# Mamba decay differences: the 0/1 triangle as the stationary tile, four heads side by side

## The chip, the cores and the metric

The kernel is one program for one core of a Trainium2 chip. The metric is the device time of one execution in microseconds (us); the runs before give 2568.35, 2570.22 and 2571.57 us, median 2570.22 us.

## The reference, cut to what matters

A network of four layers with three sublayers each (FFN, mixer, FFN) on 256 tokens of width 1024, followed by a second block of three sublayers. The mixer of the third layer is Mamba-2. Its scan works on two chunks of 128 tokens, with 32 heads in 4 groups of 8. The part that the change touches is the decay matrix of each head within a chunk:

```python
acum = jnp.cumsum(dtc * a_g, axis=1)
seg = acum[:, :, None] - acum[:, None, :]
decay = jnp.exp(jnp.where(causal, seg, -jnp.inf))
cb = jnp.einsum('blgn,bsgn->blsg', cc, bc)
y = jnp.einsum('blsg,blsgh,bsghp->blghp', cb, decay, xc * dtc[..., None])
```

For token l and source s the difference seg is the sum of dt*a over the tokens after s up to l. Written with two 0/1 triangles it is a matrix product: sum over k of [k > s] * dta[k] * [k <= l].

## The kernel before

All work runs on one core: weights come in float32 by DMA (`raw`), ScalarE rounds them to the short format float32r (`whi`, line 219), VectorE makes the remainder (`wlo`, line 222), and TensorE multiplies three times (hi*hi, hi*lo, lo*hi; lines 252 to 254 and 640 to 642). The work of each sublayer is written as steps, and a string of step names gives the order in which they are issued to a scheduler that may interleave them; buffers come from pools. For the Mamba sublayer the string is `ORDER_MAMBA` (line 114).

The Mamba steps are, for group g, chunk t and half q: `Z` (gate projection, its result `sz` stays until `Y`), `B` and `X` (projection by `feat`, lines 1012 to 1014, then the convolution `conv`: one ScalarE instruction and three on VectorE, lines 1002 and 1005), `tB` and `tX` (transposes; `tX` ends in four VectorE multiplications, line 1065), `S` (state, lines 1073 to 1077), `C` (the 128x128 matrix `cbm`, line 1085), `G` (decay, four heads at a time, lines 1087 to 1096), `Y` (output of the scan, from line 1098), `W` and `O` (output projection). `D` (line 964) computes dt and `dta` once for each chunk.

There are 16 `G` steps. Each has four VectorE instructions that scale the triangle `slow` by one head's column of `dta` into a quarter of the tile `dm`, and four float32 matmuls with that quarter as the stationary tile and the triangle `tri` as the moving one, into a quarter of the PSUM tile `pg`. The trace shows each float32 matmul as two records, each with its own weight load. ScalarE then takes the exponential of the whole `pg` back into `dm` (line 1095), and VectorE multiplies by `cbm` (line 1096). `dm` is one of the 10 buffers of the pool `half` (`NH = 10`), which `sz`, `bct`, `state`, `cacc`, `sx`, `xw`, `yi` and others share; it is held until `Y` has read it (line 1103). `pg` is one of four PSUM buffers with the tag `y`.

Of the kernel before, what the change touches and what calls it, by code (L numbers as in the profile page):

```python
# [10 lines left out]
F32 = mybir.dt.float32  # L11
F32R = mybir.dt.float32r
BF16 = mybir.dt.bfloat16
I32 = mybir.dt.int32
AF = mybir.ActivationFunctionType
OP = mybir.AluOpType
AX = mybir.AxisListType

P = 128
# [144 lines left out]
class Net:  # L164
# [783 lines left out]
    def mamba(self, x, done):  # L948
        nc, A = self.nc, self.A
# [9 lines left out]
        nc.sync.dma_start(cbb, A["ssm_conv_b"])  # L959
        ng = self.cst.tile([P, 16], F32, name="ng")  # L960
        nc.sync.dma_start(ng, A["ssm_norm_g"])
        dt, dta, ea, w, z, ys = {}, {}, {}, {}, {}, []

        def fD(t):
            if "dt" not in w:
                w["dt"] = self.wblock("ssm_w_dt", 0, 0, 1024, 32)
            ps = self.bank("mm", "pdt")
            self.lin(ps[:, :32], x, t, w["dt"], 32)
            u = self.small(32, "u")
            nc.vector.tensor_tensor(u, ps[:, :32], dtb, OP.add)  # L970
            m = self.small(32, "m")
            nc.vector.tensor_scalar(m, u, -1.0, None, op0=OP.mult)
            nc.vector.tensor_tensor(m, m, u, OP.min)
            e = self.small(32, "e")
            nc.scalar.activation(e, m, AF.Exp)
            s = self.small(32, "sden")
            nc.vector.tensor_scalar(s, e, 2.0, None, op0=OP.add)
            nc.vector.reciprocal(s, s)
            nc.vector.tensor_tensor(s, s, e, OP.mult)
            s2 = self.small(32, "s2")  # L980
            nc.vector.tensor_tensor(s2, s, s, OP.mult)
            pl = self.small(32, "pl")
            nc.vector.tensor_scalar(pl, s2, 1.0 / 19, None, op0=OP.mult)
            for k in range(17, 1, -2):
                nc.vector.scalar_tensor_tensor(pl, pl, 1.0 / k, s2, OP.add, OP.mult)
            nc.vector.scalar_tensor_tensor(pl, pl, 1.0, s, OP.add, OP.mult)
            nc.vector.tensor_scalar(u, u, 0.0, None, op0=OP.max)
            d = self.cst.tile([P, 32], F32, name=f"dt{t}")
            nc.vector.scalar_tensor_tensor(d, pl, 2.0, u, OP.mult, OP.add)
            da = self.cst.tile([P, 32], F32, name=f"dta{t}")  # L990
            nc.vector.scalar_tensor_tensor(da, d, -1.0, alog, OP.mult, OP.mult)
            dt[t], dta[t] = d, da

        def tD(t):
            pe = self.bank("tr", "pea")
# [90 lines left out]

        def fG(g, t, q):
            pg = self.bank("y", "pg").rearrange("p (a b) -> p a b", a=4)
            dm = self.half([P, 4, P], name="dm")
            for j in range(4):  # L1090
                h = 8 * g + 4 * q + j
                nc.vector.tensor_scalar(dm[:, j, :], self.slow, dta[t][:, h:h + 1], None, op0=OP.mult)
                nc.tensor.matmul(pg[:, j, :], dm[:, j, :], self.tri, start=True, stop=True)
            ee = z["e", g, t, q] = dm
            nc.scalar.activation(ee, pg, AF.Exp)
            nc.vector.tensor_tensor(ee, ee, self.bc(z["cb", g, t], 4, P), OP.mult)

# [34 lines left out]
        close = self.closers(yy, done)  # L1132
        close["E"] = close.pop("D")
        steps = dict(D=fD, tD=tD, Z=fZ, B=fB, tB=tB, X=fX, tX=tX, S=fS, C=fC, G=fG, Y=fY, W=W, O=O, **close)
        self.go(steps, ORDER_MAMBA)

# [457 lines left out]
```

## Time and profile before

| what | value |
|---|---|
| median of three runs | 2570.22 us (2568.35 to 2571.57) |
| profiled execution, span from first to last instruction | 2567.9 us, 34087 instructions |
| TensorE busy (matmul records) | 2497.5 us, 97% |
| VectorE busy | 2129.1 us, 83% |
| ScalarE busy | 1286.9 us, 50% |
| granted TensorE clock, mean | 0.992 |
| Mamba sublayer in the trace | about 1289 to 1480 us of the span |

For the profiled execution the span is all that is recorded of its time; it is 0.45 us under the lowest of the timed runs and 2.3 us under their median. A busy time counts each instruction from its start to its end, and where two overlap, once. PE is TensorE's matmuls, PEld its weight loads, DVE VectorE, ACT ScalarE.

### The profile page before, as it was taken

The page shows a single profiled execution, that of the slowest core. Times are in us where ns is not written, and L with a number is a line of the kernel's source. Part 1 is how long each engine was busy: PE and PEld are TensorE (multiplying, and loading weights), DVE is VectorE, ACT ScalarE, POOL GpSimd, SP SyncE. Part 2 cuts the span into 40 slices and gives each one's busy share as a digit, 9 for nine tenths or more (in the row PEclk, how much of TensorE's full clock was granted, in tenths as well). Part 3 has the DMA queues.
Part 4 walks back from the last instruction along what each step waited for, and adds up shares of the span by engine and source line. Part 5 has one row for each costly group of instructions (what it writes and reads, how often), then busy time and mean ns, then how long its engine had stood idle before and what let it go on. Part 6 is the DMA issues. An engine that isn't in the chain of part 4 may idle for free.

```text
span 2567.9 us, 34087 instructions
## 1 busy us (share of the span) xinstructions
PE 2497.5 (97%) x12252; PEld 2065.0 (80%) x12252; DVE 2129.1 (83%) x4847; ACT 1286.9 (50%) x2005; POOL 0.2 (0%) x4
## 2 busy tenths in 40 slices
PE   7999899999999999999999999999989999999998
PEld 6788688888887788888889778887878888788887
DVE  7888988879898988898989987698898856896754
ACT  3544474444446544544566554454446544555542
POOL 0000000000000000000000000000000000000000
PEclk9999999999999999999999999999999999999999
DMA  8888457848876388688742457658845754444552
GB/s 309 308 340 306 159 194 276 309 169 300 321 267 256 123 299 320 221 299 316 270 158 99 164 202 292 252 211 324 310 166 211 275 179 175 164 157 172 200 180 80
DMA packets 92297, 599.15 MB, mean 233 GB/s; under 512 B 12768, under 2 KB 14432, under 8 KB 24672
## 3 DMA queue, kind: packets, MB, share of 16 engines
q1 hardware_dynamic: 92128, 596.98, 63.5%
q8 instruction: 96, 1.57, 0.2%
q14 instruction: 73, 0.60, 0.1%
HBM read 593.79 MB, written 3.15 MB: 232 GB/s over the span
## 4 chain that ended last, share of the span: by engine, by line
PE 86%; DVE 7%; DMA 3%; ACT 2%; issue 1%; SPq 0%; DVEq 0%; ACTq 0%
PE tr L263 4%; PE y0q L640 3%; PE y0q L642 3%; PE y0q L641 3%; PE y1q L640 3%; PE y1q L642 3%; PE y1q L641 3%; DVE wlo L222 2%; PE hid0t L254 1%; PE hid6t L253 1%; PE hid9t L252 1%; PE hid6t L254 1%; PE hid9t L254 1%; PE hid6t L252 1%; PE hid5t L254 1%; PE hid9t L253 1%
## 5 line engine op out<-in xcount | busy, mean ns | idle before, releaser
L222 DVE TENSOR_TENSOR wlo<-raw,whi 128x384 fp32r<-128x384 f32 (+1 forms) x2385 | 1081.7, 505 | 145.8 <-ACT whi L219 76.0
L219 ACT ACTIVATE whi<-raw 128x1024 fp32r<-128x1024 f32 (+1 forms) x801 | 820.2, 1051 | 377.3 <-DMA raw<-in_ffn_w_in_dram 133.5
L371 DVE SCALAR_TENSOR_TENSOR acc<-rawm,cond,acc 128x1024 f32<-128x1024 f32 x252 | 322.9, 1281 | 13.2 <-DMA rawm<-in_w_mod_dram 8.0
L640 PE MATMUL y1q<-whi,ah 128*128 128x512 f32 x396 | 161.7, 408 | 1.7 <-ACT ah L625 1.7
L640 PE MATMUL y0q<-whi,ah 128*128 128x512 f32 x396 | 156.2, 394 | 0.7 <-ACT ah L625 0.2
L642 PE MATMUL y1q<-whi,al 128*128 128x512 f32 x396 | 156.4, 395 | 0.0
L641 PE MATMUL y0q<-wlo,ah 128*128 128x512 f32 x396 | 155.2, 392 | 0.0
L642 PE MATMUL y0q<-whi,al 128*128 128x512 f32 x396 | 155.2, 393 | 0.0
L641 PE MATMUL y1q<-wlo,ah 128*128 128x512 f32 x396 | 155.0, 391 | 0.0
L625 ACT ACTIVATE ah<-tr 128x256 fp32r<-128x256 f32 x198 | 74.7, 382 | 139.6 <-PE tr L263 136.7
L626 DVE TENSOR_TENSOR al<-tr,ah 128x256 fp32r<-128x256 f32 x198 | 82.0, 418 | 34.5 <-ACT ah L625 33.9
L640 PEld LDWEIGHTS y0q<-whi,ah 128*128 128x128 f32 x396 | 74.4, 188 | 17.1 <-ACT ah L625 2.6
L642 PEld LDWEIGHTS y1q<-whi,al 128*128 128x128 f32 x396 | 74.4, 188 | 15.7
L640 PEld LDWEIGHTS y1q<-whi,ah 128*128 128x128 f32 x396 | 74.5, 188 | 14.8 <-ACT ah L625 2.4
L642 PEld LDWEIGHTS y0q<-whi,al 128*128 128x128 f32 x396 | 74.3, 188 | 14.9 <-DVE al L626 0.2
L641 PEld LDWEIGHTS y0q<-wlo,ah 128*128 128x128 f32 x396 | 74.4, 188 | 14.5
L641 PEld LDWEIGHTS y1q<-wlo,ah 128*128 128x128 f32 x396 | 74.7, 189 | 13.2
L285 ACT ACTIVATE ev<-tr,B,G 128x128 f32<-128x128 f32 x192 | 72.9, 466 | 20.4 <-PE tr L263 20.3
L263 PEld LDWEIGHTS tr<-k_ident,ac 128*128 128x128 f32 x396 | 54.0, 140 | 29.6 <-DVE ac L616 3.0
L263 PE MATMUL tr<-k_ident,ac 128*128 128x128 f32 x396 | 74.5, 273 | 2.5 <-DVE ac L616 2.0
L295 DVE TENSOR_TENSOR tmp<-ev,tmp 128x512 fp32r<-128x512 f32 (+1 forms) x76 | 50.5, 664 | 12.7 <-ACT tmp L287 11.8
L252 PE MATMUL hid0t<-whi,tmp 128*128 128x512 f32 x144 | 56.4, 392 | 1.9 <-ACT tmp L287 1.9
(510 smaller groups left out, 6006.0 us busy)
## 6 DMA issues: line engine op xcount, KB each, us to landing
raw<-in_ffn_w_in_dram SPq DMA_DIRECT2D x176, 1024.0 KB, 4.9
rawm<-in_w_mod_dram SPq DMA_DIRECT2D x144, 1024.0 KB, 4.8
raw<-in_ffn_w_out_dram SPq DMA_DIRECT2D x88, 1024.0 KB, 5.0
raw<-in_w_gate_up_dram SPq DMA_DIRECT2D x22, 1024.0 KB, 4.7
raw<-in_w_in_dram SPq DMA_DIRECT2D x14, 1024.0 KB, 4.7
raw<-in_diff_w_in_dram SPq DMA_DIRECT2D x12, 1024.0 KB, 4.7
raw<-in_w_down_dram SPq DMA_DIRECT2D x11, 1024.0 KB, 4.7
raw<-in_w_kv_mem_dram SPq DMA_DIRECT2D x8, 1024.0 KB, 6.4
```

The costliest lines, as they stand in the source:

```text
L219: nc.scalar.activation(hi[:, q:e], s[:, q:e], AF.Copy)
L222: nc.vector.tensor_tensor(lo[:, q:e], s[:, q:e], hi[:, q:e].bitcast(F32), OP.subtract)
L252: nc.tensor.matmul(ps, xh, hi[:, off:off + n], start=first, stop=False)
L254: nc.tensor.matmul(ps, xl, hi[:, off:off + n], start=False, stop=last)
L263: self.nc.tensor.transpose(ps[:, j, :], src[:, j * P:(j + 1) * P], self.ident)
L285: nc.scalar.activation(src[:, j, :], ps[:, j, :], AF.Identity, scale=sc, bias=bcols[:, c + j:c + j + 1])
L371: nc.vector.scalar_tensor_tensor(o, src, sc, o, OP.mult, OP.add)
L625: nc.scalar.activation(ah, tr, AF.Copy)
L626: nc.vector.tensor_tensor(al, tr, ah.bitcast(F32), OP.subtract)
L640: nc.tensor.matmul(y[t][q], ah[:, k, :], hi[:, sl], start=f, stop=False)
L641: nc.tensor.matmul(y[t][q], ah[:, k, :], lo[:, sl], start=False, stop=False)
L642: nc.tensor.matmul(y[t][q], al[:, k, :], hi[:, sl], start=False, stop=l)
```

## The change

In step `G` the two operands change places and the scaling is done for four heads in one instruction. A copy of the triangle `slow` in float32r (`slowr`) is now the stationary tile. VectorE multiplies the triangle `tri`, repeated four times, by four columns of `dta`, repeated along the row, into one 128x512 float32r tile, and one 512-column matmul takes it as the moving tile. To keep precision `dta` is split into a short-format part (`dah`) and a remainder (`dal`), so there are two such multiplications and two matmuls that accumulate in `pg`, in place of four scalings and four float32 matmuls. Each of the two moving tiles is a buffer of the pool `half`, and the exponential goes to a third one. The split costs one ScalarE and one VectorE instruction on 128x32 for each chunk, the copy of the triangle one ScalarE instruction on 128x128. `slowr` and the split parts lie in a buffer that the attention of layers one and four uses for `krT`.

```diff
-        dt, dta, ea, w, z, ys = {}, {}, {}, {}, {}, []
+        both = self.fp.tile([P, 256], F32R, tag="krT", name=self.nm("both"), bufs=1)
+        slowr = both[:, :P]
+        nc.scalar.activation(slowr, self.slow, AF.Copy)
+        dt, dta, dhl, ea, w, z = {}, {}, {}, {}, {}, {}
...
-            dt[t], dta[t] = d, da
+            dah, dal = (both[:, P + 64 * t + 32 * c:P + 64 * t + 32 * c + 32] for c in range(2))
+            nc.scalar.activation(dah, da, AF.Copy)
+            nc.vector.tensor_tensor(dal, da, dah.bitcast(F32), OP.subtract)
+            dt[t], dta[t], dhl[t] = d, da, (dah.bitcast(F32), dal.bitcast(F32))
...
         def fG(g, t, q):
             pg = self.bank("y", "pg").rearrange("p (a b) -> p a b", a=4)
-            dm = self.half([P, 4, P], name="dm")
-            for j in range(4):
-                h = 8 * g + 4 * q + j
-                nc.vector.tensor_scalar(dm[:, j, :], self.slow, dta[t][:, h:h + 1], None, op0=OP.mult)
-                nc.tensor.matmul(pg[:, j, :], dm[:, j, :], self.tri, start=True, stop=True)
-            ee = z["e", g, t, q] = dm
+            hs = slice(8 * g + 4 * q, 8 * g + 4 * q + 4)
+            for i in range(2):
+                dm = self.half([P, 4, P], F32R, "dm")
+                nc.vector.tensor_tensor(dm, self.bc(self.tri, 4, P), self.hb(dhl[t][i][:, hs], 4, P), OP.mult)
+                nc.tensor.matmul(pg, slowr, dm, start=i == 0, stop=i == 1)
+            ee = z["e", g, t, q] = self.half([P, 4, P], name="ee")
             nc.scalar.activation(ee, pg, AF.Exp)
             nc.vector.tensor_tensor(ee, ee, self.bc(z["cb", g, t], 4, P), OP.mult)
```

## Rows read from the trace of the kernel before

**Rows 1.** Page, part 1: engine, busy us (share of the span), instructions.
```profile
PE 2497.5 (97%) x12252; PEld 2065.0 (80%) x12252; DVE 2129.1 (83%) x4847; ACT 1286.9 (50%) x2005; POOL 0.2 (0%) x4
```

**Rows 2.** Windows: stretch, length, busy us (count) by engine, clock, DMA share, GB/s.
```profile
1289.40:1336.30 46.90, 46.60 (x330) 43.39 (x328) 39.06 (x115) 31.97 (x41) 0.00 (x0) 0.96 0.51 180
...
1336.30:1471.40 135.10, 130.43 (x870) 115.81 (x870) 126.05 (x362) 81.42 (x120) 0.00 (x0) 1.00 0.36 126
...
1471.40:1480.00 8.60, 8.60 (x38) 7.13 (x39) 4.97 (x15) 2.06 (x4) 0.00 (x0) 1.00 0.29 118
...
1580.00:1600.00 20.00, 20.00 (x92) 16.49 (x91) 13.52 (x30) 10.68 (x14) 0.00 (x0) 1.00 0.86 322
```

**Rows 3.** Groups by shape, 1330 to 1470 us: busy, mean ns, idle before.
```profile
L1093 PE MATMUL pg<-k_tri,dm 128*128 128x128 f32 x128 | 16.1, 279 | 1.6 <-DVE dm L1092 1.6
...
L1092 DVE TENSOR_SCALAR dm<-k_slow,dta 128x128 f32<-128x128 f32 x64 | 13.2, 279 | 0.0
...
L1096 DVE TENSOR_TENSOR dm<-dm,cbm 128x512 f32<-128x512 f32 x16 | 10.5, 684 | 0.5 <-ACT dm L1095 0.4
```

**Rows 4.** Timeline of VectorE, two stretches: start, us, instruction.
```profile
1336.29 3.22 DVE L1092 TENSOR_SCALAR dm<-k_slow,dta 128x128 f32<-128x128 f32 x16
1339.42 2.49 DVE L1096 TENSOR_TENSOR dm<-dm,cbm 128x512 f32<-128x512 f32 x4
1341.94 0.48 DVE L1005 SCALAR_TENSOR_TENSOR cacc<-pbc,cw,cacc 128x253 f32<-128x253 f32 x1
...
1467.30 0.68 DVE L1104 TENSOR_TENSOR xs<-py,xs 128x512 f32<-128x512 f32 x1
...
1469.10 0.68 DVE L1110 TENSOR_TENSOR xs<-xs,yi 128x512 f32<-128x512 f32 x1
1469.70 0.42 DVE L222 TENSOR_TENSOR wlo<-raw,whi 128x256 fp32r<-128x256 f32 x1
```

**Rows 5.** Chain that ended last, first and third burst: start, us, what.
```profile
1336.62 3.84 PE pg L1093 x32
1340.46 2.63 PE py L1103 x24
...
1400.72 1.79 PE pg L1093 x16
```

**Rows 6.** Windows, a stretch of 48 short-format 512-column matmuls; columns as in Rows 2.
```profile
1455.44:1466.31 10.87, 10.87 (x49) 9.01 (x48) 9.35 (x21) 6.61 (x7) 0.00 (x0) 1.00 0.84 295
```

**Rows 7.** Chain that ended last, 1362 to 1374 us.
```profile
1365.13 1.09 PE pg L1093 x8
...
1366.24 0.61 ACT dm L1095
...
1367.76 1.56 DVE dm L1092 x8
...
1370.13 0.61 DVE dm L1096
```

**Rows 8.** Waits, 1336 to 1471 us: who waited for whom, us, times, longest.
```profile
DVE xd L1065 <- PE trx L1060: 4.2, 4, 1.9
...
DVE xs L1104 <- PE py L1103: 1.8, 4, 0.6
...
PE pg L1093 <- DVE dm L1092: 1.6, 3, 0.7
...
PE py L1103 <- DVE dm L1096: 1.4, 2, 0.7
```

**Rows 9.** Small instructions on 128x32: one line's view, and the timeline of ScalarE.
```profile
L991 DVE SCALAR_TENSOR_TENSOR dta<-dt,alog x2: 185/188/192, 1293.7 to 1307.6; 128x32 f32<-128x32 f32 x2
...
1300.77 0.22 ACT L975 ACTIVATE e<-m 128x32 f32<-128x32 f32 x1
1300.89 1.05 ACT L219 ACTIVATE whi<-raw 128x1024 fp32r<-128x1024 f32 x1
```

**Rows 10.** Timeline of ScalarE in the first burst of G steps.
```profile
1341.34 0.56 ACT L1002 ACTIVATE cacc<-pbc,cbb,cw 128x256 f32<-128x256 f32 x1 [0.24 <-DVE dm L1096]
```

## The prediction

> **What bounds the kernel now.** I read the page's engine line first. TensorE is busy 97% of the span and VectorE 83% [rows 1], so over the whole kernel a microsecond taken from TensorE could come off the time. But the change lies in one sublayer, and what it is worth is read there. So next I read the windows of the Mamba stage. Before the first `G` step TensorE is busy 46.60 of 46.90 us and VectorE 39.06. In the stretch that holds all `G` and `Y` steps, 135.10 us long, TensorE is busy 130.43 us and VectorE 126.05 us: 4.67 and 9.05 us idle, 97% and 93% [rows 2]. Here both are near their limit. ScalarE, at 81.42 us, is not. Right after it VectorE has room (4.97 of 8.60 us), and in the FFN later too (13.52 of 20) [rows 2]. [...]
>
> Then the chain that ended last. In the first burst of four `G` steps it is on TensorE: 32 records of `pg` for 3.84 us, then `py` [rows 5]. In the second it goes back and forth: `pg` 1.09 us, the exponential 0.61, eight scalings on VectorE 1.56, the multiplication by `cbm` 0.61 [rows 7]. Last the waits of the stretch: VectorE waits mostly for TensorE (4.2 us for the transposes of `tX`, 1.8 for `py`), TensorE waits for VectorE's part of `G` 1.6 and 1.4 us [rows 8]. So the two are coupled from both sides, and taking from one to give to the other is the question.
>
> **TensorE's side.** Removed: 16 steps of 8 records, 128 in all [rows 3]. Their pace is 3.84 / 32 = 0.120 us in the first burst and 1.79 / 16 = 0.112 in the third [rows 5]; the group's 16.1 us [rows 3], which also holds the tail behind each run, is the upper bound. I take 0.116, between the two bursts, so 14.8 us; bounds 14.3 to 16.1. Added: 32 short-format 512-column matmuls. The trace has the same form with another operand: 48 of them in 10.87 us, 0.226 each, weight load hidden [rows 6]. 32 x 0.226 = 7.2 us. TensorE's work falls by 7.6 us (7.1 to 8.9). The matmuls need two weight loads each step where there were eight, and loads already run beside matmuls.
>
> [...]
>
> **VectorE's side.** Removed: 64 scalings of 128x128. Sixteen in a row take from 1336.29 to 1339.42, where the next one starts: 0.196 each, 12.5 us in all [rows 4]; the group's busy time of 13.2 is the upper bound [rows 3]. Added: 32 products of two tensors on 128x512. None of the trace has both operands repeated, but one that repeats `cbm` runs at 2.52 / 4 = 0.63 us, and a run of four others at 0.60 (the first at 1467.30, the fourth at 1469.10, the next instruction at 1469.70) [rows 4]. The lone duration is 0.684 [rows 3]. I take 0.61, between the two runs: 19.5 us; bounds 19.2 (0.60) and 21.9 (0.684, nothing overlapped). The remainder `dal` adds two small ones, 0.19 each, 0.4 us [rows 9]. VectorE's work rises by 19.5 + 0.4 - 12.5 = 7.4 us (6.4 to 9.8). It nearly equals what TensorE loses.
>
> [...]
>
> **The rest.** `dah` twice and the copy of the triangle are three ScalarE instructions, each near 0.22 us [rows 9], against 53.7 us of idle ScalarE [rows 2]; cost nothing, and 0.7 us without that cover. `dal` waits for `dah` and so holds VectorE's queue, where `wlo` is next: one ScalarE cast of 1.05 us [rows 9] may stand ahead of `dah`, long before the first `G` at 1336 (`dta` is there at 1293.7 and 1307.6 [rows 9]). I count 0 to 2 us, and take 0.3. No DMA is added.
>
> **Where the sum lands.** TensorE in the stretch: 130.43 - 7.6 = 122.8. VectorE: 126.05 + 7.0 (the `dal` lie ahead of it) = 133.1 of 135.1. VectorE becomes the tighter engine, so the length follows from it: 133.1 plus the idle that remains. It was idle 9.05 us, of which at least 6.0 waiting for TensorE [rows 2, 8]. TensorE is lighter now and comes earlier, so I let half stay: 133.1 + 4.5 = 137.6, 2.5 us longer than now. Some `wlo` work of the end can slide into the 3.6 us of room behind the stretch [rows 2]; I take 1.3 us for that. With the 0.3 above it is +1.5 us. All idle kept gives +7.0, none -2.0; with the dearest product 2.8 us more. The profiled span of 2567.9 us lies 2.3 us under the median, and the sum is a difference, so 2570.2 + 1.5 = 2571.7, about 2572. Within 0.2% (5.1 us), about what a measurement of this kernel can tell from no change, this is no change.
>
> **The rivals.** *VectorE's delay goes through whole.* In each of the four bursts the four `G` steps take 8 products at 0.61 = 4.9 us before `Y` can be fed, in place of 16 scalings, 3.13: 1.7 us later four times, and the remainder of the 7.4 as late `wlo`. For it: the chain of the second burst is on VectorE [rows 7], and there and after it no room. Against: in the first burst the chain is on TensorE [rows 5], which has 2 us less to do there. It decides as soon as TensorE finds no other matmuls ready during a burst. Price +6.8 to +7.4: 2577. Chance 0.23.
>
> *TensorE's saving goes through.* The scheduler may fill the holes of VectorE, 9.05 us [rows 2], and let `wlo` slide into the FFN, where VectorE has 6.5 us of room in 20 [rows 2]. Then the stretch follows TensorE: -7.6, or about -6.5 with some waits left, 2563 to 2564. For it: 97% on TensorE in front of and behind the stretch. Against: before it too, VectorE had only 7% left. Chance 0.20.
>
> *The pool runs out.* At the first burst `half` holds, by the order string, four `sz`, `bct`, `state` and four `dm`, all ten, and the next `cacc` (1341.34) came only after `dm` work [rows 10]. The change asks for three buffers a step where there was one. Where only one is free, the second `dm` waits for the matmul of the first and the exponential for a release; some 0.5 us a step (the exponential's 0.61 [rows 7] as the measure), 8 us over 16, on top of VectorE's delay: about 2580 to 2585. Against: both `dm` are free again after a matmul. Chance 0.05.
>
> **How the numbers follow.** My forecast, the trade comes out even, gets 0.52. Slower is 0.23 + 0.05 = 0.28, faster 0.20, the same 0.52. The range reaches into both neighbours: 2564 (most of TensorE's saving) to 2580 (all of VectorE's delay and the dear product, or the start of a short pool).
>
> **What would show it.** Right: 32 `pg` matmuls at 0.23 us pace, 32 products of 0.68 us at 0.61 pace, TensorE's busy share in the stretch under 93%, VectorE's over 96%, waits of TensorE for `dm` above 3 us. Wrong: a product much dearer than 0.68 (then slower), a stretch of 128 us with VectorE's idle gone or `wlo` moved behind it (then faster), waits of ScalarE at the exponential or of VectorE at `dm` on buffers (the pool).

## The result, and the profile after

The changed kernel takes 2599.56 us (median of four runs, 2596.30 to 2604.03), the kernel before beside it 2569.28 us (2565.57 to 2571.57): ratio 1.0129, interval 1.0112 to 1.0146. It is 30 us slower. The forecast was 2572, its range ended at 2580, and "slower" had a chance of 0.28. The profiled execution has a span of 2599.4 us, and the loss is in the Mamba sublayer: the first `L528` instruction behind it starts at 1513.5 us of the span, before at 1479.0.

The page's engine line of the changed kernel, beside [rows 1]:

```profile
PE 2515.8 (97%) x12156; PEld 2073.6 (80%) x12156; DVE 2137.0 (82%) x4817; ACT 1289.2 (50%) x2008; POOL 0.2 (0%) x4
```

TensorE has 96 matmuls fewer, and its records are busy 18 us longer. The windows show where; the first two are the stretches of [rows 2].

```profile
1289.40:1336.30 46.90, 45.71 (x331) 42.83 (x331) 40.14 (x119) 33.67 (x47) 0.00 (x0) 1.00 0.51 180
1336.30:1471.40 135.10, 118.69 (x638) 98.06 (x639) 110.87 (x278) 67.54 (x101) 0.00 (x0) 0.83 0.28 95
1471.40:1506.00 34.60, 31.43 (x138) 24.47 (x137) 23.45 (x52) 13.97 (x19) 0.00 (x0) 0.89 0.39 147
```

Up to the first `G` step little differs: its first VectorE instruction starts at 1336.26 us, before at 1336.29. In the 135.1 us behind it VectorE is idle for 24.2 us where it had been for 9.05, TensorE for 16.4 where it had been for 4.67, and the granted clock is 0.83 where it was 1.00. No engine is full: this is no bottleneck moved from one engine to another, but engines that wait for each other, and a TensorE that runs part of the time at half its clock (0.50 in the windows of 4 us below). The groups of the changed instructions by shape, 1330 to 1510 us, beside [rows 3]:

```profile
L1098 DVE TENSOR_TENSOR dm<-k_tri,both 128x512 fp32r<-128x512 f32 x32 | 21.1, 688 | 1.2 <-PE pg L1099 1.2
L1099 PE MATMUL pg<-dm,both 128*128 128x512 f32 x32 | 19.3, 625 | 14.4 <-DVE dm L1098 12.6 <-DVE rv L314 1.3
...
L1101 ACT ACTIVATE ee<-pg 128x512 f32<-128x512 f32 x16 | 9.5, 598 | 38.2 <-PE pg L1099 38.1
```

A product takes 688 ns, as the row of its kind had said (684). What is new stands behind the bars: idle time ahead of the product matmuls, and 38.1 us of ScalarE ahead of the exponentials. The waits that lead, 1285 to 1520 us, beside [rows 8]:

```profile
ACT ee L1101 <- PE pg L1099: 38.1, 13, 9.6
DVE xs L1110 <- PE py L1109: 18.1, 8, 6.7
PEld pg L1099 <- DVE dm L1098: 16.3, 18, 2.3
...
PE pg L1099 <- DVE dm L1098: 12.6, 12, 1.8
```

The first of these in the kernel before, 1336 to 1471 us:

```profile
ACT dm L1095 <- PE pg L1093: 8.8, 13, 2.3
```

The first burst, beside [rows 4, 5, 10]. The timeline of VectorE (start, us, instruction, idle before and its releaser):

```profile
1336.26 3.17 DVE L1098 TENSOR_TENSOR dm<-k_tri,both 128x512 fp32r<-128x512 f32 x5
1340.11 1.29 DVE L1102 TENSOR_TENSOR ee<-ee,cbm 128x512 f32<-128x512 f32 x2 [0.68 <-ACT ee L1101]
1341.32 0.69 DVE L1098 TENSOR_TENSOR dm<-k_tri,both 128x512 fp32r<-128x512 f32 x1
1342.89 0.69 DVE L1098 TENSOR_TENSOR dm<-k_tri,both 128x512 fp32r<-128x512 f32 x1 [0.89 <-PE pg L1099]
...
1344.53 0.69 DVE L1098 TENSOR_TENSOR dm<-k_tri,both 128x512 fp32r<-128x512 f32 x1 [0.32 <-PE pg L1099]
```

That of TensorE, without the projection's matmuls ahead of it:

```profile
1337.00 3.28 PE L1099 MATMUL pg<-dm,both 128*128 128x512 f32 x5 [1.01 <-DVE dm L1098]
1342.06 0.79 PE L1099 MATMUL pg<-dm,both 128*128 128x512 f32 x1 [1.78 <-DVE dm L1098]
1343.73 0.76 PE L1099 MATMUL pg<-dm,both 128*128 128x512 f32 x1 [0.88 <-DVE dm L1098]
1344.29 3.94 PE L1109 MATMUL py<-xd,ee 128*128 128x64 f32 x18
1347.99 0.77 PE L1099 MATMUL pg<-dm,both 128*128 128x512 f32 x1
```

And that of ScalarE, from the third exponential on:

```profile
1342.89 0.60 ACT L1101 ACTIVATE ee<-pg 128x512 f32<-128x512 f32 x1 [2.33 <-PE pg L1099]
1348.80 0.60 ACT L1101 ACTIVATE ee<-pg 128x512 f32<-128x512 f32 x1 [5.31 <-PE pg L1099]
1349.29 0.56 ACT L1008 ACTIVATE cacc<-pbc,cbb,cw 128x256 f32<-128x256 f32 x1
```

Five products run in a row, in 3.17 us. The sixth starts 1.9 us after the fifth ended, behind two multiplications by `cbm` in VectorE's queue; the seventh and eighth come one at a time, each behind a matmul. Those two waits, 0.89 and 0.32 us, are all that a product waits for a matmul in the stage (the 1.2 us of the group above). The eighth's matmul stands in TensorE's queue behind 18 `py` matmuls, the last exponential behind it at 1348.80, and behind that in ScalarE's queue the convolution's `cacc`, 1349.29, in the kernel before at 1341.34 [rows 10]. TensorE reaches the next projection work, `px`, only behind `py` and `pi` in its queue. The chain that ended last has it there in the changed kernel:

```profile
1344.49 3.73 PE py L1109 x18
1348.23 0.53 PE pg L1099
1348.76 1.17 PE py L1109 x6
1349.93 1.81 PE pi L1113 x2
1351.75 0.21 PE px L1018
```

And in the kernel before, where the 24 `py` took 2.63 us [rows 5]:

```profile
1343.09 0.91 PE pi L1107 x2
1344.00 0.84 PE py L1103 x8
1344.84 0.17 PE px L1012
```

So `px` comes 6.9 us later. Of these, 3.2 us are the same `py` and `pi` matmuls (6.71 us, before 3.54). TensorE's clock in windows of 4 us:

```profile
1336.00:1340.00 4.00, 2.69 (x5) 1.13 (x5) 3.44 (x7) 2.07 (x4) 0.00 (x0) 0.85 0.61 217
1340.00:1344.00 4.00, 1.34 (x3) 0.58 (x3) 3.00 (x5) 1.17 (x3) 0.00 (x0) 0.50 0.11 45
1344.00:1348.00 4.00, 4.00 (x20) 3.90 (x19) 1.07 (x3) 0.00 (x0) 0.00 (x0) 0.50 0.02 4
1348.00:1352.00 4.00, 4.00 (x14) 2.87 (x14) 3.53 (x10) 2.07 (x5) 0.00 (x0) 0.50 0.01 2
```

TensorE was busy 2.69 and then 1.34 of 4 us, and the clock granted is 0.50, also when the 18 `py` come (3.94 us, 0.22 each; before 2.63 / 24 = 0.11 [rows 5], in a stretch at 1.00 [rows 2]). The idle time ahead of them was spent in waits for VectorE: 1.01, 1.78 and 0.88 us in the timeline of TensorE above.

### The profile page after: what moved, and what is told of

Its sections match the earlier page's. It is cut to its first block, busy times and chain, and to the rows that moved or that the text cites. A ratio compares the mean times of both kernels' runs of the same rounds, so it can differ in the third digit from the quotient of the medians.

```text
span 2599.4 us, 33868 instructions
## 1 busy us (share of the span) xinstructions
PE 2515.8 (97%) x12156; PEld 2073.6 (80%) x12156; DVE 2137.0 (82%) x4817; ACT 1289.2 (50%) x2008; POOL 0.2 (0%) x4
## 4 chain that ended last, share of the span: by engine, by line
PE 87%; DVE 8%; ACT 2%; DMA 2%; issue 1%; SPq 0%; DVEq 0%; ACTq 0%
PE tr L263 4%; PE y0q L640 3%; PE y0q L641 3%; PE y0q L642 3%; PE y1q L640 3%; PE y1q L642 3%; PE y1q L641 3%; DVE wlo L222 3%; PE hid0t L254 1%; PE hid9t L252 1%; PE hid9t L254 1%; PE hid7t L254 1%; PE hid6t L252 1%; PE hid5t L254 1%; PE hid8t L254 1%; PE hid6t L254 1%
## 5 line engine op out<-in xcount | busy, mean ns | idle before, releaser
L641 PEld LDWEIGHTS y0q<-wlo,ah 128*128 128x128 f32 x396 | 74.4, 188 | 14.4
```

The lines of the kernel that those rows point to most:

```text
L641: nc.tensor.matmul(y[t][q], ah[:, k, :], lo[:, sl], start=False, stop=False)
```

## The experiments

Two theories. *A*: the steps now draw three buffers from the pool `half` where they drew one, and the bursts run out of them. *B*: VectorE's dearer products alone. Differences are between a kernel's median and that of the kernel before in the same batch.

**Two more half buffers, in the kernel after and before.** One weight buffer pays for them.

```diff
-NR, NW, NT, NH = 3, 21, 12, 10
+NR, NW, NT, NH = 3, 20, 12, 12
```

> The changed kernel with 12 buffers in the pool half instead of 10, paid for with one weight buffer (20 instead of 21). Theory A, the pool: the 30 us are lost because three buffers a G step are asked of a full pool, so that products, matmuls and exponentials take turns and TensorE stands idle until its clock falls; two more buffers should give most of it back, 2568 to 2580 us, with the granted clock back above 0.99. Theory B, VectorE: the 7 us of dearer products, in a stage with no room, grow to 30 by themselves; then the buffers change nothing, 2592 to 2604 us.

> The kernel before with the same 12 and 20 buffers, the control for the run above. Both theories: the weights lose one buffer of 21, which may cost a little; the pool of 10 was just enough. 2565 to 2577 us.

Measured: 2613.19 (ratio 1.0176, 1.0150 to 1.0202) and 2577.42 (1.0040, 1.0023 to 1.0057); the kernel before 2566.12. A miss for both theories; the control lies 0.4 us above its range. The changed kernel stays 35.8 us above its control, and its exponentials still wait 37.5 us. So either the pool is not the cause, or two buffers more are no remedy. In this kernel no wait of a product for a matmul is left, but VectorE's queue opens the first burst in the same order:

```profile
1344.08 3.09 DVE L1098 TENSOR_TENSOR dm<-k_tri,both 128x512 fp32r<-128x512 f32 x5
1347.19 1.29 DVE L1102 TENSOR_TENSOR ee<-ee,cbm 128x512 f32<-128x512 f32 x2
```

**The products among the weight buffers.** Both product tiles lie in one buffer of the weights' pool; all instructions are those of the changed kernel.

```diff
             for i in range(2):
-                dm = self.half([P, 4, P], F32R, "dm")
+                if i == 0:
+                    d2 = self.wp.tile([P, 1024], F32R, tag="w", name=self.nm("dm"))
+                dm = d2[:, 512 * i:512 * i + 512].rearrange("p (a b) -> p a b", a=4)
```

> The changed kernel with the two product tiles of a G step in one buffer of the weights' pool (21 of 1024 columns) in place of two of the pool half, which so is asked for one buffer a step, as before the change. Theory A: near the kernel before, 2566 to 2580 us, and ScalarE's waits at the exponential back under 12 us. Theory B: 2592 to 2604 us, the products cost VectorE the same.

Measured: 2573.34, ratio 1.0027 (1.0013 to 1.0040), 7.2 us above the kernel before; the waits at the exponential are 3.5 us. Both are as A said. Of 30 us some 23 are gone without one instruction changed: what B puts on the products can't be the loss. The timeline of VectorE of this kernel shows the products of the first burst between the convolutions, from 1327.38 on:

```profile
1327.38 1.29 DVE L1100 TENSOR_TENSOR dm<-k_tri,both 128x512 fp32r<-128x512 f32 x2
...
1334.46 0.68 DVE L1100 TENSOR_TENSOR dm<-k_tri,both 128x512 fp32r<-128x512 f32 x1
```

That of TensorE shows their eight matmuls in one go:

```profile
1341.27 2.42 PE L1101 MATMUL pg<-dm,both 128*128 128x512 f32 x8
1345.16 2.89 PE L1111 MATMUL py<-xd,ee 128*128 128x64 f32 x24 [1.47 <-DVE ee L1104]
```

Its window of the stretch has the clock back at 0.99 and VectorE at 124.20 us:

```profile
1336.30:1471.40 135.10, 123.72 (x756) 105.75 (x756) 124.20 (x320) 81.39 (x120) 0.00 (x0) 0.99 0.34 125
```

**The kernel before with two half buffers a step.** The exponential goes to a buffer of its own; no instruction is dearer.

```diff
-            ee = z["e", g, t, q] = dm
+            ee = z["e", g, t, q] = self.half([P, 4, P], name="ee")
```

> The kernel before with one thing of the change alone: the exponential goes to a buffer of its own in the pool half, so a G step asks for two buffers instead of one; all instructions stay. Theory A: slower by a part of the loss, 2575 to 2595 us, with TensorE idle in the bursts. Theory B: no change, 2565 to 2575 us.

Measured: 2592.84, ratio 1.0100 (1.0079 to 1.0122), 26.7 us slower. The old arithmetic makes most of the loss by buffers alone, and shows the same picture. Its longest wait, 1285 to 1520 us:

```profile
ACT ee L1095 <- PE pg L1093: 15.6, 12, 2.9
```

TensorE's timeline of the first burst:

```profile
1341.19 2.27 PE L1093 MATMUL pg<-k_tri,dm 128*128 128x128 f32 x18 [0.61 <-DVE dm L1092]
1346.18 1.14 PE L1093 MATMUL pg<-k_tri,dm 128*128 128x128 f32 x6 [2.71 <-DVE dm L1092]
1347.79 2.05 PE L1093 MATMUL pg<-k_tri,dm 128*128 128x128 f32 x8 [0.47 <-DVE dm L1092]
```

The window of the stretch, with the clock at 0.90 and VectorE 23 us idle:

```profile
1336.30:1471.40 135.10, 123.47 (x774) 109.36 (x773) 111.81 (x331) 70.09 (x107) 0.00 (x0) 0.90 0.29 102
```

The matmuls that came as 32 in 3.84 us [rows 5] come as 18, 6 and 8 with waits for scalings between.

**One product in place of two.** This kernel leaves out the remainder's product and matmul, so that a step takes two half buffers.

```diff
-            for i in range(2):
+            for i in range(1):
...
-                nc.tensor.matmul(pg, slowr, dm, start=i == 0, stop=i == 1)
+                nc.tensor.matmul(pg, slowr, dm, start=True, stop=True)
```

> The changed kernel with only the short-format part of the values multiplied and contracted; the remainder's product and its matmul are left out (16 products of about 0.61 us and 16 matmuls of 512 columns fewer). A step then takes two half buffers in place of three. Theory A: two buffers a step still run the pool out, as in the kernel before with its exponential in a buffer of its own (2593), and VectorE's 10 us are saved beside that: 2580 to 2595, with the granted clock at half in part of the bursts. Theory B: VectorE is now 2.4 us below the kernel before, and the time is 2560 to 2570.

Measured: 2588.70, ratio 1.0083 (1.0056 to 1.0110). As A said; B's 2560 to 2570 is excluded: VectorE has some 10 us less to do than in the changed kernel, and 22 of the 30 us stay.

**The same among the weight buffers,** both edits together.

> The changed kernel with its product among the weight buffers and only the short-format part multiplied and contracted; the remainder's product and matmul are left out. Against the same kernel with both products (2573.3) it prices 16 products and 16 matmuls where no half buffer is short. Theory A (with the pool out of the way VectorE's delay goes through in full): 2573.3 less 16 x 0.61 = 2563.5. Theory B (with the pool out of the way the products are hidden and VectorE's time no longer counts): 2571 to 2575.

Measured: 2571.69, ratio 1.0019 (1.0007 to 1.0031), against 1.0027 (1.0013 to 1.0040) with both products. The intervals overlap: 16 products of 0.61 us, 9.8 us of VectorE, are worth 7.2 - 4.9 = 2.3 us, not told apart from nothing; the two intervals together allow some 7 us at most (an estimate), not 9.8. The expectation's A (2563.5) is a miss and B (2571 to 2575) holds: where the buffers suffice, the products do not go through whole.

**The old arithmetic with that room.** The kernel before, its scalings in a weight buffer, its exponential in a half buffer.

```diff
-            dm = self.half([P, 4, P], name="dm")
+            dm = self.wp.tile([P, 1024], F32R, tag="w", name=self.nm("dm"))[:, :512].bitcast(F32).rearrange("p (a b) -> p a b", a=4)
...
-            ee = z["e", g, t, q] = dm
+            ee = z["e", g, t, q] = self.half([P, 4, P], name="ee")
```

> The kernel before with its four scaled triangles in a weight buffer and the exponential in a half buffer of its own; every instruction's operation is that of the kernel before. One half buffer a step, as before, and room to make the triangles early. Theory A (the change's arithmetic is an even trade, what counts is where the tiles lie): 2563 to 2573, level with the changed kernel whose products lie among the weights (2573.3) or up to 8 us below it. Theory B (the change's arithmetic gains once the pool is out of the way): 2578 to 2590, slower than the changed kernel with its products there.

Measured: 2570.78, ratio 1.0010 (0.9998 to 1.0023), not told apart from the kernel before. With equal room the new arithmetic (7.2 us above the kernel before) stands 3.2 us above the old one (4.0), with overlapping intervals. That fits an even trade, and by the intervals also a loss of 7 us.

**Two buffers of the products' own,** paid for with one weight buffer.

```diff
-NR, NW, NT, NH = 3, 21, 12, 10
+NR, NW, NT, NH = 3, 20, 12, 10
...
-                dm = self.half([P, 4, P], F32R, "dm")
+                dm = self.fp.tile([P, 4, P], F32R, tag="dm", name=self.nm("dm"), bufs=2)
```

> The changed kernel with its two product tiles in two buffers of their own, and one weight buffer fewer (20 in place of 21, which costs the room). The half pool then gives one buffer a step, as before the change. Theory A (the burst runs out of half buffers because the products draw on them): only two products can be made ahead of their matmuls, but the exponential no longer waits for half buffers behind the steps of its own burst; if what counts is that products can be made early, as they were where they lay among the weights (2573), two buffers do not allow it, and the time stays at 2590 to 2605; if what counts is only who holds the half buffers, it falls to 2570 to 2582. Theory B (the dearer products on VectorE alone): no change against the changed kernel, 2595 to 2605.

Measured: 2589.50, ratio 1.0087 (1.0072 to 1.0102), 22.7 us above the kernel before. It lies 0.5 us under A's first case, that products must be made early, and looked like it. But the weight buffer's price is in it, and this reading did not hold, as the next kernels show.

**Four such buffers, with both products and with one, and controls for the weight buffers.** `bufs=4` with 19 weight buffers; the same with the remainder's product and matmul left out; the kernel before with 19; the kernel before and after with 20.

> The changed kernel with its product tiles in four buffers of their own, two steps' worth, and 19 weight buffers in place of 21. Its control is the kernel before with 19 weight buffers, in the same batch. Theory A (the loss is set by how many steps' products can be made ahead of their matmuls): between one step ahead (2589.5, 22 us above the kernel before) and the room of the weight buffers (6 to 7 us above it): 10 to 17 us above the control. Theory B (what counts is that no other tile shares the buffers, and the depth does not matter): as with two buffers, 20 to 25 us above the control.

> The same with the remainder's product and its matmul left out, so that the four buffers are four steps' worth, a whole group's. Theory A: level with the weight buffers, 0 to 7 us above the control. Theory B: as the two buffers less the 10 us of VectorE that the products left out took, 10 to 16 us above the control.

> The control: the kernel before with 19 weight buffers in place of 21, nothing else. From the kernel with 20 weight buffers and 12 half buffers (10 us slower, most of it taken to be the weights'): 5 to 25 us above the kernel before under both theories.

> The control for the kernels with 20 weight buffers: the kernel before with 20 in place of 21, nothing else. Theory A (depth): the weight buffer costs little here, 0 to 4 us, so that the two buffers of the products' own stay some 20 us above their control. Theory B (sharing): it costs 8 to 14 us, as the 12 half buffers with 20 weight buffers did, so that the two own buffers are 9 to 14 us above it, level with the four own buffers (11 us above theirs).

> The changed kernel with 20 weight buffers, nothing else; against the same with 12 half buffers (2613) it tells what the two more half buffers did. If they helped at all: above 2613, to 2625. If they did nothing and the weight buffer made the loss: 2608 to 2614. If the weight buffer costs nothing in the changed kernel and the two half buffers made it worse: 2597 to 2605.

| kernel | us | ratio (interval) | above the kernel before | above its control |
|---|---|---|---|---|
| four own buffers, 19 weights | 2599.86 | 1.0114 (1.0093 to 1.0135) | 30.8 | 11.3 |
| the same, one product | 2596.98 | 1.0102 (1.0081 to 1.0124) | 28.0 | 8.4 |
| before, 19 weights | 2588.57 | 1.0070 (1.0050 to 1.0091) | 19.5 | control |
| before, 20 weights | 2576.35 | 1.0048 (1.0029 to 1.0066) | 8.3 | control |
| after, 20 weights | 2611.34 | 1.0174 (1.0157 to 1.0191) | 43.3 | 35.0 |

A weight buffer costs the kernel before 8 us, the next 11 more. Against the control with 20, the two own buffers are 22.7 - 8.3 = 14.4 above it, and four are 11.3 above theirs: the depth makes little difference. Theory A of these expectations, depth, met its number for four buffers, but it rested on 22 us for two, and with the control for 20 weight buffers (8.3 us, as B had it there) that premise is gone. With one product, four buffers hold a whole group's, and 8.4 us remain, between the ranges of the two theories. And 12 half buffers in the changed kernel are 35.8 us above their control where 10 are 35.0: two more changed nothing that can be measured. What helped wherever it was tried is that the products do not draw on the pool of the exponentials at all. With four own buffers the wait at the exponential has shrunk from 38.1 us to

```profile
ACT ee L1101 <- PE pg L1099: 4.6, 3, 4.2
```

**The clock apart from the waiting.** Four matmuls on a tile that lies ready, ahead of each step's first product matmul; the second kernel does it with the products among the weights.

```diff
+                if i == 0:
+                    for _ in range(4):
+                        nc.tensor.matmul(pg[:, :2, :], slowr, both.rearrange("p (a b) -> p a b", a=2), start=True, stop=True)
                 nc.tensor.matmul(pg, slowr, dm, start=i == 0, stop=i == 1)
```

> The changed kernel with four matmuls of 256 columns (the stationary triangle on a tile that lies ready since the start of the stage) ahead of each step's first product matmul, into the bank that this matmul then overwrites; they wait for no product and give TensorE something to do while it would wait. At half of the 0.226 us of 512 columns they are some 0.45 us a step and 7 us in all. Theory A1 (most of the lost 30 us is the clock that falls to 0.50 when TensorE waits for products): the granted clock of the bursts is back above 0.9 and the time falls by 8 to 20 us, to 2580 to 2592, in spite of the added matmuls. Theory A2 (the loss is the turn-taking for buffers itself; the half clock costs little because TensorE waits anyway): the clock may rise, but the time stays at 2597 to 2608.

> The control of the one before: the changed kernel with its products among the weight buffers (2573.3), with the same four added matmuls a step. It prices the added matmuls where the clock stays up. TensorE is busy nearly throughout the stage there, so they go through: 2573.3 + 7 = 2580; a hidden share would leave 2573 to 2578.

Measured: 2596.12, ratio 1.0112 (1.0095 to 1.0129), and 2574.94, ratio 1.0031 (1.0020 to 1.0042). The control's added matmuls are hidden (2573.34 without them, intervals overlapping). In the first kernel the mean clock of the profiled span rose from 0.983 to 0.990, and the time, 1.0129 before, did not measurably fall. Of 270 windows of 0.5 us over the changed kernel's stretch the clock is 1.00 in 172 and 0.50 in 90, with 8 between. As an estimate, if every stretch of the span is at full or at half speed, a mean of 0.983 is 2 x 0.017 x 2599 = 88 us at half, one of 0.990 is 2 x 0.010 x 2593 = 52: 36 us fewer at half speed, for 1 us by the differences to the kernel before (30.3 and 29.1) or 4 by the ratios. A1's time is a miss, and A2's range (2597 to 2608) is missed by 0.9 us. The run does not decide, for its condition was not met: in the first burst the fillers did not come where TensorE waits. Its timeline shows 16 in one go, ahead of the products:

```profile
1336.47 2.47 PE L1101 MATMUL pg<-both 128*128 128x256 f32 x16
1338.78 0.40 PE L1102 MATMUL pg<-dm,both 128*128 128x512 f32 x1
```

They stand on the chain that ended last themselves:

```profile
1337.03 1.91 PE pg L1101 x16
```

From 1340 to 1360 us the clock is 0.74, in the changed kernel 0.69. So the fillers put work on the chain while they raised the clock, and do not tell what the lower clock costs. The chain of the changed kernel shows that it costs something: the 3.2 us of `py` and `pi` in the first burst. A bound, as an estimate: at 0.83, 2 x 0.17 x 135.1 = 46 us of the stretch ran at half, which is 23 us lost if TensorE was on the chain in all of them. How much of the 30 us it is stays open.

**The remainder's product on GpSimd,** with the products among the weights.

```diff
-                nc.vector.tensor_tensor(dm, self.bc(self.tri, 4, P), self.hb(dhl[t][i][:, hs], 4, P), OP.mult)
+                (nc.gpsimd if i else nc.vector).tensor_tensor(dm, self.bc(self.tri, 4, P), self.hb(dhl[t][i][:, hs], 4, P), OP.mult)
```

> The changed kernel with its products among the weight buffers, and the remainder's product made on GpSimd, which is idle in the stage, in place of VectorE (16 products of 0.61 us less there). Theory A (VectorE's time counts in the stage): as with the remainder left out, some 2 to 9 us below 2573.3, 2564 to 2572. Theory B (GpSimd's products come later than VectorE's did, and TensorE waits for them): 2575 to 2590.

Measured: 2580.14, ratio 1.0043 (1.0023 to 1.0063), 13.1 us above the kernel before where VectorE's products had 7.2: slower or the same, not faster, in B's range. Its group on GpSimd (the idle time is of the whole run up to there):

```profile
L1100 POOL TENSOR_TENSOR dm<-k_tri,both 128x512 fp32r<-128x512 f32 x16 | 19.8, 1256 | 1416.8 <-PE pdt L254 1303.1 <-DVE cacc L1011 53.5 <-DVE wlo L222 34.8
```

1.256 us a product, 1.8 times VectorE's 0.688.

## Why the prediction was wrong

*TensorE's and VectorE's instructions: right.* A product takes 0.688 us alone and five run in 3.17 us, a pace of (3.17 - 0.69) / 4 = 0.62 where 0.61 was taken. `dah` and `dal` take 0.226 and 0.190 us; the first product starts at 1336.26, the first scaling had at 1336.29 [rows 4], so the loss does not lie ahead of the first `G`. The eight matmuls of a burst take 2.42 us from the first's start to the last's end where buffers suffice, 0.6 more than 8 x 0.226 = 1.8.

*"The trade comes out even": not refuted as arithmetic.* With room for the products the change lies 3.2 us above the old arithmetic with the same room, +1.5 in the sum; the intervals overlap and do not tell +1.5 from +7.

*The step that failed* is "Where the sum lands": it took the length of the stretch as VectorE's work plus half of the idle time it had before (4.5 us). The idle time was 24.2 us. The sum priced instructions and gave no price to what the diff does to the pool, three buffers a step in place of one.

*The rival "The pool runs out"* named the pool and the place. The waits at the exponential appeared, but for `pg`, its input (38.1 us), and products waited for a matmul, which frees a buffer, only 1.2 us. It was mis-sized in price and chance: 0.5 us a step, 8 us over 16, chance 0.05. Half buffers drawn a step, against the nearest control:

| half buffers a step | kernels | us above the control |
|---|---|---|
| 1, products elsewhere | old arithmetic among the weights; new among the weights; four own; two own | 4.0; 7.2; 11.3; 14.4 |
| 1, one product, elsewhere | among the weights; four own | 4.9; 8.4 |
| 2 | old arithmetic; new with one product | 26.7; 21.9 |
| 3 | the change; with 20 weights; with 12 half buffers | 30.3; 35.0; 35.8 |

The second buffer takes most of the loss, whatever the arithmetic; the third adds little. The price was off because it counted one wait of one exponential a step. In the trace the first burst alone brings `px` 6.9 us late: products come late in VectorE's queue, the eighth's matmul stands behind 18 `py`, and at half the clock `py` and `pi` take 3.2 us more. The "against" of that rival, that both `dm` are free again after a matmul, was true and no help: the matmul itself came late.

*The clock has no term in the sum.* In the stretch it is 1.00 in the kernel before [rows 2] and 0.83 in the changed one. What that costs is not nothing, 3.2 us in the first burst; the whole price was not measured.

*"VectorE's delay goes through whole"* (2577) is not borne out: 9.8 us of VectorE left out were worth 2.3 us where there was room. That the change with room lies 7.2 us up, the price of this rival, is no proof of it: the old arithmetic in that room lies 4.0 us up. "TensorE's saving goes through" found no support in any run.

*Open:* how the tiles drawn from `half` delay the work: the products' own waits are small (1.2 us), and where the products lie changes the order in VectorE's queue (five and then two multiplications by `cbm`, or all eight between the convolutions), so a rival, that the scheduler's order makes the loss, was not tested apart; why own buffers leave 8 to 14 us above their controls where the weights' room leaves 7; which tiles of `half` are released late (the records show who is waited for, not which buffer was handed out); why two more half buffers did nothing. That the exponentials are held until `Y` has read them, and so block the pool, fits the table but is argued, not shown.

## What to carry to other kernels

Count the buffers that a step takes from a shared pool before and after an edit: an edit in the costs of instructions that also turns one tile into two or three is first an edit of the pool, and here the second buffer alone cost 27 us with no instruction dearer. To tell buffers from arithmetic, give the old arithmetic the new buffers and the new arithmetic other buffers; here these two runs told them apart. A wait in the trace need not be for the buffer itself: compare the order of the queues too. Where a buffer is paid for with another, run the kernel before with the same payment: without the control with 20 weight buffers, two own buffers looked like a different cause.

## What was not expected of the hardware

The clock fell to 0.50 in the first burst, with TensorE busy 1.34 of 4 us, and stayed there through 18 matmuls at 0.22 us each, against 0.11 in the kernel before, at 1.00 [rows 2, 5]. On the chain that ended last this made the 24 `py` and two `pi` of that burst 3.2 us longer. Giving TensorE more to do brought the mean clock from 0.983 to 0.990 without a measurable gain, but the added matmuls stood on the chain themselves: a mean clock does not tell what the clock costs.
